# One Strassen level for the gate and up products of two SwiGLU FFNs

## The chip, the core and the metric

The kernel runs on one core of one Trainium2 chip. TensorE (PE) multiplies matrices and writes PSUM, VectorE (DVE), ScalarE (ACT) and GpSimd (POOL) work element by element, SyncE (SP) issues the DMA transfers. The metric is the device time of one execution in microseconds, as the median of several runs.

## What is computed

An inference step of a two-layer decoder: a pooling mixer and an FFN, then a gated DeltaNet mixer and an FFN, each between two RMS norms, on 512 prompt tokens and 64 sample tokens together (T = 576) with 1024 features. The change is about the FFN of both layers:

```python
def swiglu(h, w_in, w_out):
    gu = h @ w_in                                  # 1024 x (2 x 2816)
    return (jax.nn.silu(gu[..., :D_FF]) * gu[..., D_FF:]) @ w_out

for i in range(DEPTH):
    h = rms_norm(x, norm_mix_pre[i])
    ...
    x = x + rms_norm(m, norm_mix_post[i])
    h = rms_norm(x, norm_ffn_pre[i])
    x = x + rms_norm(swiglu(h, ffn_w_in[i], ffn_w_out[i]), norm_ffn_post[i])
```

## The kernel before

**Layout.** Activations lie with features on the 128 partitions (8 chunks) and tokens along the free dimension. The tokens are cut into two halves (`HALVES`): A with 256 columns and B with 320, with PSUM banks 0 to 2 and 3 to 5 (tags A and B, so `ps_A` and `ps_B`).

**Arithmetic.** Every large product is made of three matmuls on float32r: an operand is split into a rounded part (`wh`, `hH`, `aH`, made by an ACT copy) and the rest (`wl`, `hL`, `aL`, a subtraction on DVE or GpSimd). `mm3` (L663) adds wh x hH, wh x hL and wl x hH for each chunk. `Weights` (L645) loads a block of 1024 x 128 weights as one DMA into `wraw` (three slots) and splits it into `wh` and `wl` (three slots each).

**The FFN** (`ffn`, L759). The hidden layer has 22 slices of 128, in blocks of 8, 7 and 7 (`FBLOCKS`). A slice is a pair: a gate block and an up block of w_in, 8 chunks each. A block's slices are followed by eight output tiles (`y`), products with w_out that are summed over the blocks. The first pairs of each FFN, its head (14 chunks, 7 pairs, in layer 0, 10 chunks, 5 pairs, in layer 1), run for half A and then again for half B, with the weights loaded twice, since B's norm is not done yet; the last eight output tiles do likewise, so that A's norm can begin before B is done. Between them each weight block is used for both halves. The residual x stays in SBUF through each FFN; in layer 1 it is transposed on PE beside the pairs (`turn_x`, L1721) into `xT`, to which the turned output is added.

**Between the layers** x goes to DRAM (`x_d`), since the mixer of layer 1 needs its room. That mixer's output product is made in two parts: the first is put away in DRAM (`y_d`), the second is added behind the mixer (L1699 to L1710), where `y_d` and `x_d` come back in one transfer for each half.

**The order.** The kernel's calls are not issued as they are written. `Plan` (L51) records them with their dependences, and `forward` (L339) sets an order for each engine from estimated durations, several times over with changed priorities; the best is issued. An operation marked `EITHER` goes to DVE or GpSimd. Where the planner expects PE to wait for long it puts fillers there, matmuls on ones into an unused bank (`ps_w`, issued at L279; two records each in the trace). On its engine each queue runs in order; SP's DMA issues too. All recorded operations have one line in the profile, L283.

Of the kernel before, what the change touches and what calls it, by code (L numbers as in the profile page):

```python
# [11 lines left out]
F32 = mybir.dt.float32  # L12
# [38 lines left out]
class Plan:  # L51
# [16 lines left out]
    LEAVE, KEEP = 0.3, 1.0  # L68
    ROUNDS, STIR, SEED = 40, (0.0, 0.0, 300.0, 1000.0, 3000.0), 2
# [4 lines left out]
    def start(self):  # L74
        self.on = True
        self.ops, self.last, self.tags = [], {}, {}
        self.gone, self.ends, self.home, self.after = set(), set(), {}, {}
        self.banks, self.holds = {}, {}

    class Engine:  # L80
        def __init__(self, plan, real):
            self.plan, self.real = plan, real

        def __getattr__(self, method):
            def put(*a, **k):
# [47 lines left out]
    @staticmethod  # L133
    def meet(a, b):
        return a[0] < b[1] and b[0] < a[1] and a[2] & b[2] != 0

# [51 lines left out]
    def put(self, method, calls, a, k):  # L188
# [10 lines left out]
        for x, write in [(x, False) for x in ins] + [(x, True) for x in outs]:  # L199
# [20 lines left out]
            for q, w in log:  # L220
                if (write or w) and q[0] != i and self.meet(r, q[1]):
                    preds.add(q[0])
            log.append(((i, r), write))
# [115 lines left out]
    def forward(self, rank):  # L339
# [65 lines left out]
        while todo:  # L405
# [23 lines left out]
            if e == "POOL":  # L429
# [5 lines left out]
                if not mine:  # L435
# [4 lines left out]
                    continue  # L440
            elif e == "DVE" and port["POOL"] > t + 300:
# [57 lines left out]
def hybrid_kernel(  # L499
# [12 lines left out]
        ("PE", nc.tensor), ("ACT", nc.scalar), ("DVE", nc.vector), ("POOL", nc.gpsimd), ("SP", nc.sync)))  # L512
    EITHER = plan.engine(DVE=nc.vector, POOL=nc.gpsimd)
# [41 lines left out]
    hv = [None, None]  # L555

    def new_h(hi):
        hv[hi] = [hp.tile([P, NC, HALVES[hi][1]], F32R, name="h%s%d" % (x, hi), tag="h%s%d" % (x, hi), bufs=1)
                  for x in "HL"]

    for hi in range(2):
        new_h(hi)
# [4 lines left out]


    sp = pool("gsmp")

    bet = sp.tile([P, SP1, VH], F32, name="bet")
    gH = sp.tile([P, SP1, VH], F32R, name="gH")
    gL = sp.tile([P, SP1, VH], F32R, name="gL")
    gce = sp.tile([P, SP1, VH], F32, name="gce")
    gcq = sp.tile([P, SP1, VH], F32, name="gcq")
    ngc = sp.tile([P, SP1, VH], F32, name="ngc")
    kde = sp.tile([P, SP1, VH], F32, name="kde")
    gls = sp.tile([P, NB, VH], F32, name="gls")
    glp = sp.tile([P, SPANS, VH], F32, name="glp")
    rq = sp.tile([P, SP1, KH], F32, name="rq")  # L580
    nk = sp.tile([P, SP1, KH], F32, name="nk")
# [63 lines left out]
    class Weights:  # L645
# [98 lines left out]
    def pre_norm(tp, x, acc, hi, gpre, on_dve=False):  # L744
        o0, n = HALVES[hi]
        r = rstd(tp, acc, hi, on_dve)
        for c in range(NC):
            t = halftile(tp, "nh", hi, 2)
# [4 lines left out]
    def post_pre(tp, x, m, acc, hi, gpost, gpre, fast=False):  # L753
        acc2 = []
        post_norm(tp, x, m, acc, hi, gpost, acc2, (DVE, POOL) if fast else (POOL,), hi == 1)
        pre_norm(tp, x, acc2, hi, gpre, hi == 1)


    def ffn(layer, y, wts, ap_, tp, head, tail, finish, beside=None, turn=None):  # L759
# [3 lines left out]
        chunks = []  # L763
        f0 = 0
        for bi, nb in enumerate(FBLOCKS):
            for f in range(nb):
                chunks.append(("g", bi, f, f0, nb))
                chunks.append(("u", bi, f, f0, nb))
            for m in range(NC):
                chunks.append(("y", bi, m, f0, nb))  # L770
            f0 += nb
# [1031 lines left out]
```

## Time and profile before

| what | value |
| --- | --- |
| median of 3 runs | 1650.28 us |
| their range | 1646.72 to 1653.22 us |
| span of the profiled execution (its own time is given as this alone) | 1654.1 us |
| mean granted clock of PE over the span | 0.989 |

A line of the profile names an engine, an operation and its tiles (written <- read), with buffer numbers left out. PE's matmuls overlap, so their pace is read from start to start. The stages by time: pooling mixer and norms to about 60 us, FFN of layer 0 to about 490, mixer of layer 1 to about 1140, its output product to about 1190, FFN of layer 1 to the end.

### The profile page before, as it was taken

How to read it: one execution, taken by the hardware profiler on the slowest of the kernel's cores; microseconds unless marked ns; L12 is line 12 of the kernel's file. 1: busy time of each engine (PE TensorE's matmuls, PEld its weight loads, DVE VectorE, ACT ScalarE, POOL GpSimd, SP SyncE). 2: the span in 40 equal slices, each digit the busy share in tenths (PEclk: the TensorE clock that was granted, in tenths of full speed). 3: DMA queues.
4: the chain of work that ended last, by engine and by line, in shares of the span. 5: the costliest groups of instructions: out<-in, count | busy, mean ns of one | idle time of the engine just before them, and what ended most of it. 6: DMA issues, size and time to landing. Idle time of an engine off the chain costs nothing. (4 is left out here: it accounts for less than half of the span.)

```text
span 1654.1 us, 30525 instructions
## 1 busy us (share of the span) xinstructions
PE 1620.4 (98%) x12317; PEld 1567.2 (95%) x12317; DVE 1002.7 (61%) x2074; ACT 699.4 (42%) x1434; POOL 119.5 (7%) x265
## 2 busy tenths in 40 slices
PE   8999999999999999999999999999999999999997
PEld 8999999999999998998898899899999999999997
DVE  6784223333387798997998899656694312233244
ACT  6653233212365944553453554424464322222244
POOL 3010000000001010021121131100000000000000
PEclk8899999999999999999999999999999999999999
DMA  6255322223366233324323423557544323223333
GB/s 175 67 157 146 90 77 81 86 77 90 92 171 167 84 104 93 100 75 137 89 77 104 116 78 116 163 167 244 171 135 135 102 75 92 72 79 92 87 102 113
DMA packets 329812, 185.25 MB, mean 112 GB/s; under 512 B 12235, under 2 KB 324140, under 8 KB 329407
## 3 DMA queue, kind: packets, MB, share of 16 engines
q1 hardware_dynamic: 329671, 183.30, 38.2%
q8 instruction: 97, 1.59, 0.4%
q14 instruction: 44, 0.36, 0.1%
HBM read 157.73 MB, written 25.77 MB: 111 GB/s over the span
## 5 line engine op out<-in xcount | busy, mean ns | idle before, releaser
L283 DVE TENSOR_TENSOR wl<-wraw,wh 128x1024 fp32r<-128x1024 f32 (+2 forms) x253 | 301.9, 1201 | 292.1 <-PE ps_A L283 102.6
L283 ACT ACTIVATE wh<-wraw 128x1024 fp32r<-128x1024 f32 (+2 forms) x259 | 266.4, 1035 | 481.5 <-PE ps_A L283 185.9
L283 PE MATMUL ps_m<-hH,wh 128*128 128x256 f32 (+1 forms) x832 | 239.1, 309 | 1.4 <-ACT zz L283 1.2
L283 PE MATMUL ps_m<-hL,wh 128*128 128x256 f32 (+1 forms) x832 | 238.9, 308 | 0.0
L283 PE MATMUL ps_m<-hH,wl 128*128 128x320 f32 (+1 forms) x832 | 236.7, 309 | 0.0
L283 PE MATMUL ps_B<-hL,wh 128*128 128x320 f32 x768 | 224.2, 311 | 0.3 <-DVE hL L283 0.3
L283 PE MATMUL ps_B<-hH,wl 128*128 128x320 f32 x768 | 223.9, 311 | 0.1
L283 PE MATMUL ps_B<-hH,wh 128*128 128x320 f32 x768 | 223.3, 311 | 0.3 <-ACT sg L283 0.3
L283 PE MATMUL ps_A<-hH,wh 128*128 128x256 f32 x768 | 205.6, 285 | 1.3 <-DVE yo L283 1.3
L283 PE MATMUL ps_A<-hL,wh 128*128 128x256 f32 x768 | 204.1, 284 | 0.0
L283 PE MATMUL ps_A<-hH,wl 128*128 128x256 f32 x768 | 202.7, 284 | 0.1
L283 PEld LDWEIGHTS ps_m<-hH,wh 128*128 128x128 f32 x832 | 152.5, 190 | 6.5 <-ACT zz L283 1.8
L283 PEld LDWEIGHTS ps_m<-hL,wh 128*128 128x128 f32 x832 | 152.5, 190 | 2.2 <-DVE hL L283 0.2
L283 PEld LDWEIGHTS ps_m<-hH,wl 128*128 128x128 f32 x832 | 151.8, 190 | 2.8 <-issue 0.9
L283 PEld LDWEIGHTS ps_A<-hH,wh 128*128 128x128 f32 x768 | 142.8, 191 | 2.3 <-issue 1.4
L283 PEld LDWEIGHTS ps_A<-hL,wh 128*128 128x128 f32 x768 | 142.7, 191 | 0.2
L283 PEld LDWEIGHTS ps_A<-hH,wl 128*128 128x128 f32 x768 | 141.8, 191 | 0.4 <-DVE wl L283 0.2
L283 PEld LDWEIGHTS ps_B<-hL,wh 128*128 128x128 f32 x768 | 141.2, 189 | 0.6 <-DVE hL L283 0.5
L283 PEld LDWEIGHTS ps_B<-hH,wl 128*128 128x128 f32 x768 | 141.2, 189 | 0.5 <-DVE wl L283 0.2
L283 PEld LDWEIGHTS ps_B<-hH,wh 128*128 128x128 f32 x768 | 140.4, 189 | 0.9 <-ACT sg L283 0.5
L283 PE MATMUL ps_B<-aH,wh 128*128 128x320 f32 x352 | 102.1, 311 | 0.0
L283 PE MATMUL ps_B<-aL,wh 128*128 128x320 f32 x352 | 102.0, 310 | 0.0
(388 smaller groups left out, 3109.1 us busy)
## 6 DMA issues: line engine op xcount, KB each, us to landing
wraw<-in_ffn_w_in_dram SPq DMA_DIRECT2D x112, 512.0 KB
wraw<-in_gdn_w_in_dram SPq DMA_DIRECT2D x56, 512.0 KB
wraw<-in_ffn_w_out_dram SPq DMA_DIRECT2D x48, 448.0 KB
wraw<-in_gdn_w_out_dram SPq DMA_DIRECT2D x24, 512.0 KB
wraw<-in_ffn_w_out_dram SPq DMA_DIRECT2D x16, 512.0 KB
St<-in_state_gdn_rec_dram SPq DMA_DIRECT2D x32, 256.0 KB
out_dram<-St SPq DMA_DIRECT2D x32, 256.0 KB
z_d<-zz SPq DMA_DIRECT2D x16, 288.0 KB
```

The source lines that it names most:

```text
L283: calls[e](*a, **k)
```

## The change

**Products.** The tokens are also cut into two equal parts N1 and N2 of 288 columns, the features into two halves K1 and K2 of four chunks. Behind the heads, whose sizes stay, a pair is seen as a 2 x 2 block matrix (gate and up by K1 and K2) times a 2 x 2 block matrix (K1 and K2 by N1 and N2). `seven` multiplies them by the Strassen-Winograd scheme with seven block products (`part`, four chunks of three matmuls on 288 columns each) in three PSUM banks. The sums of weights that it needs are made for each pair from the raw weights and split like weights: `ws` (split into `wh`, `wl`), the changed up block (`th`, `tl`, one slot) and half of the changed gate block (`qh`, `ql`, one slot). The sums of results are added on DVE between the products: `su` is up, `sg` gate.

**Activations.** The sums of activations are made once for each FFN: `twist` writes them over the normed activations, which `pre_norm` now leaves in y, and splits them into `tH` and `tL` (`TW`). `hH` and `hL` become one tile for both halves.

**x.** `tH` takes x's place in SBUF. So x goes to a DRAM tile `x_m` before the pairs and comes back for the last pass; in layer 1 its transposition moves there too, and `xT` takes the place of `tL`.

**Transfers.** x and y move in pieces by feature chunk. Those marked `BULK` wait in the planner while it expects the DMA queue to be over `QUEUE` further behind. The small tiles of the mixer of layer 1 (`gsmp`) exist during that mixer only.

```diff
+N1, N2 = slice(0, T // 2), slice(T // 2, T)
+K1, K2 = slice(0, NC // 2), slice(NC // 2, NC)
+HEADS = (7, 5)
...
+            elif e == "SP" and dma > t + 1400 + self.QUEUE:
+                mine = [x for x in q if not taken[x[1]] and x[1] not in self.bulk]
+                if not mine:
+                    soon = [r[0][0] for r in (ready[e],) if r and r[0][0] > t]
+                    free[e] = max(t + 50.0, min(soon + [dma - 1400 - self.QUEUE]))
...
+    HT = [hp.tile([P, NC, T], F32R, name="h%s" % x) for x in "HL"]
+    hv = [[h[:, :, o0:o0 + n] for h in HT] for o0, n in HALVES]
+    x_m = dp.tile([P, NC, T], F32, name="x_m")
...
-        def load(self, src, row, col, nk, n=P, eng=EITHER):
+        def raw_of(self, src, row, col, nk, n=P):
             raw = self.p.tile([P, 8, P], F32, name="wraw", tag="wraw", bufs=self.raw)[:, :nk, :n]
             SP.dma_start(raw, src[row:row + nk * P, col:col + n].rearrange("(k p) m -> p k m", p=P))
-            return self.split(raw, eng)
-
-        def split(self, raw, eng=EITHER):
+            return raw
+
+        def load(self, src, row, col, nk, n=P, eng=EITHER):
+            return self.split(self.raw_of(src, row, col, nk, n), eng)
+
+        def split(self, raw, eng=EITHER, p=None, tag="w", bufs=None):
             _, nk, n = raw.shape
-            h = self.p.tile([P, 8, P], F32R, name="wh", tag="wh", bufs=self.bufs)[:, :nk, :n]
-            l = self.p.tile([P, 8, P], F32R, name="wl", tag="wl", bufs=self.bufs)[:, :nk, :n]
+            full = 8 if p is None else nk
+            h, l = ((p or self.p).tile([P, full, P], F32R, name=tag + x, tag=tag + x, bufs=bufs or self.bufs)[:, :nk, :n]
+                    for x in "hl")
...
+    def twist(Y, TW):
+
+        for a, b in ((0, 2), (2, 4)):
+            top, low = Y[:, a:b], Y[:, 4 + a:4 + b]
+            EITHER.tensor_tensor(top[:, :, N1], top[:, :, N2], top[:, :, N1], op=sub)
+            EITHER.tensor_tensor(top[:, :, N2], low[:, :, N2], top[:, :, N2], op=sub)
+            EITHER.tensor_tensor(low[:, :, N2], low[:, :, N2], top[:, :, N1], op=sub)
+            EITHER.tensor_tensor(low[:, :, N1], low[:, :, N1], low[:, :, N2], op=sub)
+            for c in range(a, b):
+                for k in (c, 4 + c):
+                    split2(Y[:, k], TW[0][:, k], TW[1][:, k])
...
+        def part(ps, w, k0, src, ks, cols, first):
+            wh, wl = w
+            for j, k in enumerate(range(ks.start, ks.stop)):
+                hi_, lo = (t[:, k, cols] for t in src)
+                PE.matmul(ps, wh[:, k0 + j], hi_, start=first and j == 0, stop=False, skip_group_check=True)
+                PE.matmul(ps, wh[:, k0 + j], lo, start=False, stop=False, skip_group_check=True)
+                PE.matmul(ps, wl[:, k0 + j], hi_, start=False, stop=j == 3, skip_group_check=True)
+
+        def seven(f, ring):
+
+            rg, ru = (wts.raw_of(*win_of(kind, f)) for kind in "gu")
+            w0 = wts.split(rg)
+            ws = ap_.tile([P, 8, P], F32, name="ws", tag="ws", bufs=1)
+            EITHER.tensor_tensor(ws[:, K1], ru[:, K1], ru[:, K2], op=add)
+            EITHER.tensor_tensor(ws[:, K2], ws[:, K1], rg[:, K1], op=sub)
+            w1 = wts.split(ws)
+            EITHER.tensor_tensor(ru[:, K1], rg[:, K1], ru[:, K1], op=sub)
+            w2 = wts.split(ru, p=ap_, tag="t", bufs=1)
+            EITHER.tensor_tensor(rg[:, K2], rg[:, K2], ws[:, K2], op=sub)
+            w3 = wts.split(rg[:, K2], p=ap_, tag="q", bufs=1)
+            a, b, c = (bank(ring)[:, :T // 2] for _ in range(3))
+            sg = ap_.tile([P, T], F32, name="sg", tag="sg", bufs=2)
+            u = ap_.tile([P, T], F32, name="su", tag="su", bufs=2)
+            part(a, w0, 0, HT, K1, N1, True)
+            ACT.activation(u[:, N1], a, AF.Copy)
+            part(c, w1, 0, TW, K1, N1, True)
+            part(b, w1, 4, TW, K2, N2, True)
+            DVE.tensor_tensor(sg[:, N2], u[:, N1], b, op=add)
+            part(a, w0, 4, HT, K2, N1, False)
+            ACT.activation(sg[:, N1], a, AF.Silu)
+            part(b, w2, 0, TW, K1, N2, False)
+            DVE.tensor_tensor(u[:, N2], u[:, N1], b, op=add)
+            DVE.tensor_tensor(u[:, N2], u[:, N2], c, op=add)
+            part(c, w3, 0, HT, K2, N2, False)
+            DVE.tensor_tensor(sg[:, N2], sg[:, N2], c, op=add)
+            ACT.activation(sg[:, N2], sg[:, N2], AF.Silu)
+            part(b, w2, 4, TW, K2, N1, False)
+            DVE.tensor_tensor(u[:, N1], u[:, N1], b, op=add)
+            gated(f, sg, u, slice(0, T))
...
+        for hi in range(2):
+            for f in range(head):
+                plain(f, hi)
+        for bi, (f0, nb) in enumerate(blocks):
+            for f in range(max(f0, head), f0 + nb):
+                seven(f, "AB"[f % 2])
+            if bi == last:
                 ACT.activation(warm, eps_c, AF.Sqrt)
-            if i == len(chunks) - 1:
-                finish(hi, s["acc"])
-
-        n = len(chunks)
-        last_silu = n - NC - 2
-        for lo, hi in ((0, head), (n - tail, n)):
-            if lo:
-                for i in range(head, lo):
-                    w = load(i)
-                    run(i, 0, w)
-                    run(i, 1, w)
-                    if beside is not None and i >= 2 * head:
-                        next(beside, None)
-            for half in range(2):
-                for i in range(lo, hi):
-                    run(i, half, load(i))
+                more = back()
+                for hi in range(2):
+                    for m in range(NC):
+                        for _ in range(2):
+                            next(more, None)
+                        out(bi, m, hi, wts.load(wout, f0 * P, m * P, nb))
+            else:
+                for m in range(NC):
+                    w = wts.load(wout, f0 * P, m * P, nb)
+                    for hi in range(2):
+                        out(bi, m, hi, w)
...
+                for c in range(NC):
+                    BULK.dma_start(x_m[:, c, o0:o0 + n], x[:, c, o0:o0 + n])
...
+            TW = [xp.tile([P, NC, T], F32R, name="tH", tag="x", bufs=1), ap_.tile([P, NC, T], F32R, name="tL")]
+            twist(Y, TW)
+            xs = []
+
+            def back0():
+                x = xp.tile([P, NC, T], F32, name="x", tag="x", bufs=1)
+                xs.append(x)
+                for o0, n in HALVES:
+                    for c in range(NC):
+                        BULK.dma_start(x[:, c, o0:o0 + n], x_m[:, c, o0:o0 + n])
+                return iter(())
...
-    for hi, (o0, n) in enumerate(HALVES):
-        SP.dma_start(y[o0], y_d[hi])
     for hi, (o0, n) in enumerate(HALVES):
         acc = []
         for m in range(NC):
+            BULK.dma_start(y[o0][:, m], y_d[hi][:, m])
+            BULK.dma_start(x[:, m, o0:o0 + n], x_d[:, m, o0:o0 + n])
             ps = bank("AB"[hi])[:, :n]
-            if m == 3:
-                SP.dma_start(x[:, :, o0:o0 + n], x_d[:, :, o0:o0 + n])
             mm3(ps, wts.load(wo, 8 * P, m * P, 8), h_of(hi), 8)
             yc = y[o0][:, m]
             DVE.tensor_tensor(yc, yc, ps, op=add)
             add_sq(tp, acc, yc, m, hi)
-        new_h(hi)
         post_pre(tp, x, y, acc, hi, G_MPOST + NC, G_FPRE + NC, True)
+        for c in range(NC):
```

The whole order is planned anew. Three places of it, without row numbers.

DVE, in the middle of layer 0's pairs (`wl` and `wraw` of one pair, `sg` and `aL` of the pairs whose products are done). Before, the operations of one pair's length:

```order
L283 TENSOR_TENSOR wl_697<-wraw_695,wh_696 128x1024
L283 TENSOR_TENSOR sg_663<-sg_663,ps_B_672 128x320
L283 TENSOR_TENSOR aL_674<-sg_663,aH_673 128x320
L283 TENSOR_TENSOR wl_706<-wraw_704,wh_705 128x1024
L283 TENSOR_TENSOR sg_680<-sg_680,ps_A_688 128x256
L283 TENSOR_TENSOR aL_690<-sg_680,aH_689 128x256
```

Now, from the last reader of a raw slot (`ql_665` reads `wraw_655`) to the sums of the next pair (`wraw_676` gate, `wraw_677` up, which is loaded into the slot of `wraw_655`):

```order
L295 TENSOR_TENSOR ql_665<-wraw_655,qh_664 128x512
L295 TENSOR_TENSOR sg_672<-su_673,ps_B_669 128x288
L295 TENSOR_TENSOR tl_663<-wraw_656,th_662 128x1024
L295 TENSOR_TENSOR su_652<-su_652,ps_A_648 128x288
L295 TENSOR_TENSOR sg_651<-sg_651,su_652 128x576
L295 TENSOR_TENSOR ws_680<-wraw_677 128x512
L295 TENSOR_TENSOR ws_680<-ws_680,wraw_676 128x512
L295 TENSOR_TENSOR su_673<-su_673,ps_B_669 128x288
L295 TENSOR_TENSOR wraw_676<-wraw_676,ws_680 128x512
L295 TENSOR_TENSOR su_673<-su_673,ps_B_671 128x288
L295 TENSOR_TENSOR wl_682<-ws_680,wh_681 128x1024
L295 TENSOR_TENSOR wraw_677<-wraw_676,wraw_677 128x512
```

Behind these follow, up to the next `ql`, a 576-wide `aL`, a 1024-wide `wl`, a 288-wide `sg` and `ql` itself: 15 operations from one `ql` to the next, all on DVE, where six stood before.

PE, within one pair now (`ps_B_625`, `627` and `629` are its banks a, b and c):

```order
L295 MATMUL ps_B_629<-tL_336,wh_618 128x288
L295 MATMUL ps_B_625<-hH_97,wh_615 128x288
L295 MATMUL ps_B_629<-tH_335,wl_619 128x288
L295 MATMUL ps_B_625<-hL_98,wh_615 128x288
L295 MATMUL ps_B_625<-hH_97,wl_616 128x288
L295 MATMUL ps_B_625<-hH_97,wh_615 128x288
L295 MATMUL ps_B_627<-tH_335,th_620 128x288
L295 MATMUL ps_B_627<-tL_336,th_620 128x288
```

Bank b is written again here (`ps_B_627<-tH_335,th_620`), which waits for the addition `sg_630<-su_631,ps_B_627` on DVE; between the two uses of the bank PE has the other products.

SP, where the FFN of layer 1 is entered (`yo` and `x1` come back, `wraw` are blocks of the output weights). Before:

```order
L283 DMA wraw_2825<-in_gdn_w_out_dram 128x8x128
L283 DMA yo0_2787<-y_d0_104 128x2048
L283 DMA yo256_2788<-y_d256_105 128x2560
L283 DMA x1_2789<-x_d_101 128x8x256
L283 DMA x1_2789<-x_d_101 128x8x320
L283 DMA wraw_2831<-in_gdn_w_out_dram 128x8x128
L283 DMA wraw_2837<-in_gdn_w_out_dram 128x8x128
```

Now:

```order
L295 DMA wraw_2799<-in_gdn_w_out_dram 128x8x128
L295 DMA wraw_2793<-in_gdn_w_out_dram 128x8x128
L295 DMA yo_2750<-y_d0_103 128x256
L295 DMA wraw_2825<-in_gdn_w_out_dram 128x8x128
L295 DMA yo_2750<-y_d0_103 128x256 x7
L295 DMA yo_2750<-y_d256_104 128x320 x3
L295 DMA x1_2751<-x_d_100 128x256 x4
L295 DMA wraw_2831<-in_gdn_w_out_dram 128x8x128
```

The two blocks that stood behind the four transfers (half A's last two) stand ahead of the first piece, and the pieces have half B's weight loads between them. The order has 102 fillers before and 86 now; here the 3, 20, 26 and 2 become 20, of the others 51 become 66.

More of the change, by code (lines that the diff above doesn't have):

```diff
@@ L135, in meet, with inside @@
         return a[0] < b[1] and b[0] < a[1] and a[2] & b[2] != 0
+    @staticmethod
+    def inside(a, b):
+        return b[0] <= a[0] and a[1] <= b[1] and a[2] & ~b[2] == 0
     @staticmethod
@@ L222, in put @@
                     preds.add(q[0])
+            if write and x.space == SB:
+                log[:] = [q for q in log if not self.inside(q[0][1], r)]
             log.append(((i, r), write))
@@ L755, in post_pre @@
         post_norm(tp, x, m, acc, hi, gpost, acc2, (DVE, POOL) if fast else (POOL,), hi == 1)
[L756 to L781 removed]
+        pre_norm(tp, x, acc2, hi, gpre, m, hi == 1)
@@ new lines, in ffn, with win_of, act_of, gated @@
+    def ffn(layer, y, wts, ap_, tp, head, TW, back, finish, turn=None):
+        win, wout = ffn_w_in[layer], ffn_w_out[layer]
+        blocks, f0 = [], 0
+        for nb in FBLOCKS:
+            blocks.append((f0, nb))
+            f0 += nb
+        last = len(blocks) - 1
+        state = [dict(acc=None, turn=None) for _ in HALVES]
+        acts = {}
+        def win_of(kind, f):
+            return win, 0, (f if kind == "g" else DFF // P + f) * P, NC
+        def act_of(f):
+            if f not in acts:
+                acts[f] = [ap_.tile([P, T], F32R, name="a" + x, tag="a" + x, bufs=8) for x in "HL"]
+            return acts[f]
+        def gated(f, sg, u, cols):
+            aH, aL = (a[:, cols] for a in act_of(f))
+            DVE.tensor_tensor(sg, sg, u, op=mult)
+            ACT.activation(aH, sg, AF.Copy)
+            EITHER.tensor_tensor(aL, sg, aH.bitcast(F32), op=sub)
+        def plain(f, hi):
+            o0, n = HALVES[hi]
+            cols = slice(o0, o0 + n)
+            sg = ap_.tile([P, T], F32, name="sg", tag="sg", bufs=2)[:, cols]
+            for kind in "gu":
+                ps = bank("AB"[hi])[:, :n]
+                mm3(ps, wts.load(*win_of(kind, f)), h_of(hi), NC)
+                if kind == "g":
+                    ACT.activation(sg, ps, AF.Silu)
+            gated(f, sg, ps, cols)
+        def part(ps, w, k0, src, ks, cols, first):
[35 more added lines that the diff above has]
+            gated(f, sg, u, slice(0, T))
+        def out(bi, m, hi, w):
+            f0, nb = blocks[bi]
@@ new lines, in out @@
+            yc = y[o0][:, m]
+            if bi == 0:
+                ACT.activation(yc, ps, AF.Copy)
+            else:
+                DVE.tensor_tensor(yc, yc, ps, op=add)
+            if bi == last:
+                if m == 0:
+                    s["acc"] = []
+                add_sq(tp, s["acc"], yc, m, hi)
+                if turn is not None:
+                    if s["turn"] is not None:
+                        next(s["turn"], None)
+                    s["turn"] = turn(hi, m)
+                    next(s["turn"])
+                    if m == NC - 1:
+                        next(s["turn"], None)
+                if m == NC - 1:
+                    finish(hi, s["acc"])
```

140 lines of the change are left out of this document (56 added, 84 removed).

## The prediction

> **What bounds the kernel now.** I read the page first, for the engine that is full.
>
> ```profile
> span 1654.1 us, 30525 instructions
> PE 1620.4 (98%) x12317; PEld 1567.2 (95%) x12317; DVE 1002.7 (61%) x2074; ACT 699.4 (42%) x1434; POOL 119.5 (7%) x265
> PE   8999999999999999999999999999999999999997
> DVE  6784223333387798997998899656694312233244
> ```
>
> The first two lines are the span and the busy times; the slices show that TensorE (PE) is full from end to end, while VectorE (DVE) is full only in the middle, in the mixer of layer 1. Next I read the stretches that the change touches, beside that mixer (600 to 1050 us).
>
> ```profile
> core 0: us, PE busy (x) PEld busy (x) DVE busy (x) ACT busy (x) POOL busy (x), PEclk, DMA share, GB/s
> 60.00:150.00 90.00, 89.67 (x659) 88.41 (x659) 64.17 (x125) 46.49 (x77) 4.41 (x5) 0.98 0.49 143
> 200.00:450.00 250.00, 250.00 (x1886) 250.00 (x1885) 76.99 (x113) 67.56 (x107) 0.00 (x0) 1.00 0.28 81
> 600.00:1050.00 450.00, 434.50 (x3583) 402.85 (x3582) 405.86 (x961) 213.99 (x531) 69.28 (x139) 0.99 0.35 99
> 1200.00:1250.00 50.00, 49.95 (x390) 48.98 (x389) 45.66 (x101) 31.53 (x56) 3.54 (x3) 1.00 0.47 138
> 1300.00:1550.00 250.00, 250.00 (x1881) 249.83 (x1881) 75.91 (x110) 66.96 (x109) 0.00 (x0) 1.00 0.29 85
> 1600.00:1650.00 50.00, 45.69 (x332) 42.96 (x330) 28.68 (x49) 26.73 (x51) 0.00 (x0) 1.00 0.38 116
> ```
>
> Behind the heads of both FFNs (200 to 450, 1300 to 1550) PE never idles, the granted clock is 1.00, and DVE works 30% of the time. There fewer or shorter matmuls are worth their whole time, until something else fills up. 250 us over 1886 matmuls is 132.6 ns each, start to start.
>
> **The pair: PE.** A pair is the gate and up column block for one 128-wide slice of the hidden layer. Before, it takes 2 x 8 x 3 matmuls on 256 columns and as many on 320, 96 in all. Now seven products of 4 x 3 matmuls on 288 columns, 84. No row has 288 columns; the neighbours in the timeline do:
>
> ```profile
> 250.03 0.28 PE L283 MATMUL ps_A<-hH,wh 128*128 128x256 f32 x1
> 250.15 0.31 PE L283 MATMUL ps_B<-hL,wh 128*128 128x320 f32 x1
> 250.30 0.28 PE L283 MATMUL ps_A<-hL,wh 128*128 128x256 f32 x1
> 250.42 0.31 PE L283 MATMUL ps_B<-hH,wl 128*128 128x320 f32 x1
> ```
>
> From a start (first column) to the next is 0.12 us after 256 columns and 0.15 after 320. 288 lies halfway, so I take the mean of the stage, 132.6 ns: 96 x 0.1326 = 12.73 us before, 84 x 0.1326 = 11.14 after, 1.59 less. Heads of 7 and 5 pairs stay as they are, so 15 + 17 = 32 pairs change: **-50.9 us**. With the ends of the bracket, 0.12 and 0.15, a pair would save 2.65 or 0.13 us, 85 or 4 in all; the straight line is why I stay at the middle.
>
> The Trainium skill (TensorE: Matmul & The Clock Gate, Back-to-back issue gap) gives N/2.4 + 2.5 ns for a warm matmul by itself, 122.5 at 288 columns; the same edit would then be worth 32 x 12 x 0.1225 = 47 us. At 256 columns it gives 109 ns where the trace has 0.12 us, so the measurement stands.
>
> **The pair: DVE.** This is the price. Before, DVE does six operations a pair (two weight residuals, two multiplications, two residuals of the activations). Now 15, by the order: three on 1024 elements (wl twice, tl), five on 512 (four sums of weights, ql), five on 288 with PSUM, two on 576. All stand on DVE, none on GpSimd.
>
> ```profile
> L283 DVE TENSOR_TENSOR wl<-wraw,wh 128x1024 fp32r<-128x1024 f32 x204 | 249.7, 1231 | 276.7 <-PE ps_A L283 95.6 <-ACT wh L283 59.8 <-issue 33.1
> L283 DVE TENSOR_TENSOR St<-St,ps_s 128x512 f32<-128x512 f32 x32 | 21.6, 682 | 2.1 <-PE ps_s L283 1.9
> L283 DVE TENSOR_TENSOR sg<-sg,ps_B 128x320 f32<-128x320 f32 x44 | 21.3, 485 | 80.0 <-PE ps_B L283 79.9
> L283 DVE TENSOR_TENSOR sg<-sg,ps_A 128x256 f32<-128x256 f32 x44 | 18.4, 418 | 70.8 <-PE ps_A L283 70.8
> 1142.09 3.49 DVE L283 TENSOR_TENSOR wl<-wraw,wh 128x1024 fp32r<-128x1024 f32 x3
> L283 ACT ACTIVATE wh<-wraw 128x1024 fp32r<-128x1024 f32 x210 | 221.3, 1058 | 393.3 <-PE ps_A L283 134.8 <-PE ps_B L283 102.5 <-PE ps_m L283 68.1
> L283 ACT ACTIVATE aH<-sg 128x320 fp32r<-128x320 f32 x44 | 20.7, 470 | 41.6 <-DVE sg L283 41.4
> ```
>
> The mean ns of one stands behind the busy time: 1231, 682, and between 485 and 418 the 452 of 288 columns; 576 on the line from 512 to 1024 is 751. Sum: 3 x 1.231 + 5 x 0.682 + 5 x 0.452 + 2 x 0.751 = 10.86 us. The row at 1142.09 shows three operations of 1.23 us in 3.49 us, so the next one starts about 0.1 us before the last one's end: 15 of them take 9.4 us back to back. So **DVE fills 84 to 97% of PE's 11.14 us**, where it was at 30%. On ACT a pair has 3.5 weight copies of 1024 elements (3.5 x 1.058 = 3.7 us), three short operations like the 0.470 row and one of 576: under 6 us, half of the pair.
>
> The Trainium skill (VectorE: DVE Perf Modes, The DRAIN you can't avoid) states that the next operation does not start until the pipe is empty; by that a pair would cost DVE the full 10.86 us. The 3.49 us row speaks against it.
>
> Two things make DVE wait as well. The raw weights have three slots and a pair holds two of them, so the load of the next up block is issued only after ql, the last reader of the slot. How long a load takes is seen here:
>
> ```profile
> 261.61 0.37 SPq L283 DMA_DIRECT2D wraw<-in_ffn_w_in_dram  x1
> 264.00:264.50 0.50, 0.50 (x6) 0.50 (x5) 0.00 (x0) 0.00 (x0) 0.00 (x0) 1.00 1.00 300
> 264.50:265.00 0.50, 0.50 (x6) 0.50 (x5) 0.00 (x0) 0.27 (x1) 0.00 (x0) 1.00 0.13 37
> ```
>
> Issued at 261.6, its bytes have come by 264.6 (share 1.00, then 0.13): 3.0 us. Meanwhile DVE has, by the order, sg, tl, su and sg, 0.45 + 1.23 + 0.45 + 0.75 = 2.9 us. Then the whole chain of sums stands behind the load, and behind it on the same in-order queue the additions on PSUM for which PE waits before it may write that bank again. So engine and load turn once in 3.0 + about 0.4 for issue and waking + (9.4 to 10.9 - 2.9) = 9.9 to 11.4 us, beside PE's 11.14: level with it. What PE loses beside so full a DVE two rows tell: 0.05 of 50 us where DVE is at 91% (1200 to 1250), 15.5 of 450, 3.4%, where it is at 90% and often full (600 to 1050). The handshakes resemble the second: 3.4% of 32 x 11.14 = 356 us is **+12 us**; ends 0.4 and, if DVE sets the pace, the second rival below.
>
> **The entry into layer 1's FFN.** Here y and x come back from DRAM in four big transfers before, in 32 pieces now.
>
> ```profile
> 1142.49 0.83 PE L279 MATMUL ps_w<-ones 128*128 128x128 f32 x6
> 1146.11 4.62 PE L279 MATMUL ps_w<-ones 128*128 128x128 f32 x40
> 1152.02 0.35 PE L283 MATMUL ps_A<-hH,wh 128*128 128x256 f32 x1 [1.28 <-DVE yo L283]
> 1160.72 5.96 PE L279 MATMUL ps_w<-ones 128*128 128x128 f32 x52
> 1166.76 0.61 PE L279 MATMUL ps_w<-ones 128*128 128x128 f32 x4
> 1143.94 1.09 SPq L283 DMA_DIRECT2D yo<-y_d  x2
> 1145.08 6.25 SPq L283 DMA_DIRECT2D x<-x_d  x2
> 1151.45 1.08 DVE L283 TENSOR_TENSOR yo<-yo,ps_A 128x256 f32<-128x256 f32 x3 [1.61 <-DMA yo<-y_d]
> ```
>
> ps_w are fillers, matmuls on ones where the planner expects PE to wait. PE loses 0.83 + 4.62 + 1.28 + 5.96 + 0.61 = 13.3 us: first for y, issued at 1143.94 and there at 1151.4, then for weights queued behind x. In the order the 20 fillers (40 records) stay, the 26 (52) go, and all of this half's weights are issued ahead of the first piece of y. Elsewhere, above all in layer 1's mixer, which is planned anew with the rest though no line of its arithmetic changes, the order has 66 fillers for 51, 15 x 2 x 0.1155 = 3.5 us (4.62 us over 40 records is 0.1155). So 13.3 - 4.6 - 3.5: **-5 us**. Ends: -13 if the pieces come early and the rest waits less, 0 if they delay weights instead.
>
> **The transfers of x and the twist.** The twist adds 16 DVE operations on 576 (12 us) and 8 ACT copies in each head; in 60 to 150 DVE has 26 us idle, which hides it; without this cover it costs up to 12. x goes to DRAM in the head and comes back in the last pass: 2.36 MB each way, at the 300 GB/s of the row above 8 us, while the DMA share there is 0.49 and 0.38. On SP's in-order queue the return waits for the last pair's matmuls to release its slot; the loads of wout for the remaining tiles stand behind, PE waits for them, and the four or five wout blocks issued ahead cover it. I take **+2 us**, ends 0 and 28 (12 + 2 x 8, both heads' and returns' cover gone).
>
> **Sum.** 1654.1 - 50.9 + 12.3 - 5 + 2 = 1612.5 us. The profiled execution's own time is given as its span only; it lies 0.23% above the median of the runs, so on their scale 1612.5 x 1650.28/1654.1 = **1608 us**.
>
> **Rivals.**
> - *The gain comes whole* (PE loses 0.4, the entry 13, no cost elsewhere): 1654.1 - 50.9 + 0.4 - 13 = 1590.6, 1587 on the runs' scale. For: 49.95 of 50 beside a DVE at 91%. Against: three slots, one loop. 0.08.
> - *DVE sets the pace.* Full durations 10.86, 0.5 for the load, 0.8 for two hand-overs from ACT: 12.2 us a pair, saving 0.53 x 32 = 17: 1654.1 - 17 - 5 + 2 = 1634, 1630. For: 97% by full durations. Against: the overlap in the 3.49 us row. 0.18. The DRAIN rule of the Trainium skill would lead here.
> - *The transfers and the twist lose their cover*: +28 in place of +2: 1638.5, 1635. 0.08.
> - *Slower: the slot loop.* If a load takes longer than 3.0 us, DVE stands still and PE behind it. With 3.0 us the loop is at most 11.4; it passes the old 12.73 when the load takes over 4.3 us. At 5 us it is 13.4, 0.67 x 32 = 21 us more: 1654.1 + 21 - 5 + 2 = 1672, 1668. For: y took 7.4 us when much was queued. Against: the DMA share in this stage is 0.28. 0.10.
> - The forecast has 0.56.
>
> The change does do what it says: the order has 84 matmuls a pair.
>
> **Range and chances.** 1592 to 1642 leaves out the slower rival and half of the first. What a measurement of this kernel can tell from no change is about 0.5%, 8 us. Faster: 0.56 + 0.08 + 0.16 + 0.06 = 0.86; within: 0.05; slower: 0.09.
>
> **What would show it.** Right: a stretch of pairs with 84 matmuls in 11.2 to 11.7 us, DVE busy 85 to 97%, PE waits of some tenths of a us for DVE's su, sg, tl or wl; the 52 filler records gone. Wrong: 288 columns pacing off 0.13 us; DVE waiting on wraw's DMA for over 1 us a pair; PE waiting for x or wout in the last passes; PE's clock below 1.00 in the pairs.

## The result, and the profile after

| | before | after |
|---|---|---|
| median of 4 runs each | 1649.63 us (1646.72 to 1653.22) | 1608.78 us (1607.29 to 1609.98) |
| ratio | | 0.9749, 95% interval 0.9732 to 0.9765 |
| span of the profiled execution | 1654.1 us | 1605.2 us |
| mean granted clock of PE | 0.989 | 0.989 |

The first lines of the page of the changed kernel, with the slices of PE and DVE:

```profile
span 1605.2 us, 30246 instructions
PE 1567.4 (98%) x11901; PEld 1509.0 (94%) x11901; DVE 1210.6 (75%) x2392; ACT 768.5 (48%) x1516; POOL 130.5 (8%) x267
PE   8999999999999999999999899999999999999998
DVE  6995368568785896997999699757598835846865
```

PE is as full as before with 416 fewer records of matmuls (384 are the pairs' own, 32 x 12, and 32 are fillers), and DVE is now busy in all stages. The stretches that the prediction looked at, in the changed kernel (time from and to; length, then busy time of PE, PEld, DVE, ACT and POOL with instructions; granted clock, DMA share, GB/s):

```profile
60.00:150.00 90.00, 89.20 (x660) 87.61 (x660) 70.77 (x129) 48.37 (x78) 11.14 (x9) 1.00 0.56 163
200.00:450.00 250.00, 249.87 (x1886) 248.52 (x1885) 175.60 (x267) 103.42 (x154) 1.23 (x2) 1.00 0.37 107
1300.00:1550.00 250.00, 250.00 (x1885) 248.96 (x1885) 164.68 (x246) 98.52 (x147) 0.00 (x0) 1.00 0.33 94
```

Behind the heads PE still hardly idles (0.13 us of 500), and its pace is what it was: 1886 and 1881 matmuls in 250 us before, 1886 and 1885 now, though most of them now have 288 columns in place of 256 and 320.

To see where the time went I cut both executions at the same instructions: FFN of layer 0 (first matmul into ps_A on hH to the first into ps_e), mixer of layer 1 (first to last matmul into ps_m), and the last stage (from there to the end, with the FFN of layer 1). The three windows of the kernel before:

```profile
59.10:493.80 434.70, 434.25 (x3238) 432.43 (x3238) 191.95 (x329) 156.08 (x254) 6.86 (x8) 0.99 0.37 106
528.80:1134.60 605.80, 589.57 (x4668) 549.75 (x4667) 515.81 (x1195) 299.69 (x729) 81.33 (x161) 0.99 0.38 109
1134.60:1654.10 519.50, 509.44 (x3833) 504.14 (x3831) 226.37 (x389) 185.32 (x319) 8.55 (x8) 1.00 0.38 113
```

and of the changed one:

```profile
56.40:465.70 409.30, 408.37 (x3049) 404.82 (x3050) 285.57 (x466) 180.42 (x285) 16.73 (x17) 1.00 0.42 122
500.00:1119.60 619.60, 601.09 (x4717) 557.85 (x4716) 520.88 (x1213) 308.32 (x741) 74.45 (x153) 0.99 0.38 108
1119.60:1605.20 485.60, 475.17 (x3560) 469.65 (x3559) 333.68 (x551) 220.56 (x356) 13.07 (x12) 0.99 0.44 130
```

The FFN of layer 0 lost 25.4 us (15 pairs at 1.59 are 23.9) and the last stage 33.9 (17 pairs are 27.0; 6.9 more). So the two FFN stages gained 59 us. But **the mixer of layer 1, of which no line of arithmetic is changed, takes 13.8 us longer**. The rest of the span (ahead of the FFN, and the product into ps_e) gave 3.4. These windows come from one execution each: that of the kernel before, with its span of 1654.1 us, lies above all four runs, that of the change is the fastest of its four, so the spans differ by 48.9 us where the medians differ by 40.9. Two questions followed: what the pairs cost beyond their matmuls, and what lengthened the mixer.

In the mixer PE has 49 more records. These two rows are the fillers in it, before and (second fence) after:

```profile
L279 PE MATMUL ps_w<-ones 128*128 128x128 f32 x42 | 6.0, 280 | 0.0
```

```profile
L291 PE MATMUL ps_w<-ones 128*128 128x128 f32 x64 | 9.1, 275 | 0.0
```

22 of the 49 are fillers, 19 are products for the gates that moved over the stage's border. At the stage's pace, 601.09 / 4717 = 0.127 us, the 49 are 6.2 us; PE's idle time grew from 16.2 to 18.5. The granted clock has a share in the other 5.3. In the mixer it falls to 0.50 for short stretches: two before (606.23 to 609.65 and 770.07 to 776.90 us), 10.2 us together, three after (545.73 to 552.56, 617.41 to 620.82, 893.89 to 900.72), 17.1 us. The first of the three with the time behind it, matmuls from both, and (last fence) the longer one before:

```profile
545.73:552.56 6.83, 6.83 (x25) 5.70 (x26) 6.10 (x11) 6.73 (x11) 0.47 (x2) 0.50 0.28 77
552.56:559.39 6.83, 6.83 (x44) 6.35 (x43) 4.97 (x17) 5.16 (x9) 0.00 (x0) 1.00 0.11 43
```

```profile
549.37 0.41 PE L295 MATMUL ps_m<-hH,wh 128*128 128x256 f32 x1
549.58 0.41 PE L295 MATMUL ps_m<-hL,wh 128*128 128x256 f32 x1
...
552.57 0.28 PE L295 MATMUL ps_m<-hL,wh 128*128 128x256 f32 x1
552.69 0.28 PE L295 MATMUL ps_m<-hH,wl 128*128 128x256 f32 x1
```

```profile
770.07:776.90 6.83, 6.83 (x102) 6.37 (x99) 1.98 (x3) 1.42 (x3) 0.52 (x1) 0.50 0.55 156
```

Inside it matmuls on 256 columns start 0.21 us apart, just behind it 0.12. Half the length of such stretches is an estimate of what they cost, 5.1 us before and 8.5 after, so 3.4 of the 13.8. The clock is not a fixed part of an order: 50 executions of the kernel before, beside the experiments, took 1645.99 to 1660.54 us at clocks between 0.999 and 0.987. The last 2 us stay without a name. Whether the order is what differs, the runs with other orders tell (below).

### The profile page after: what moved, and what is told of

Same layout as the page of the kernel before. It is cut to its first block, busy times and chain, and to the rows that moved or that the text cites. A ratio compares the mean times of both kernels' runs of the same rounds, so it can differ in the third digit from the quotient of the medians.

```text
span 1605.2 us, 30246 instructions
## 1 busy us (share of the span) xinstructions
PE 1567.4 (98%) x11901; PEld 1509.0 (94%) x11901; DVE 1210.6 (75%) x2392; ACT 768.5 (48%) x1516; POOL 130.5 (8%) x267
## 4 chain that ended last, share of the span: by engine, by line
PE 74%; DVE 15%; ACT 4%; DMA 4%; issue 2%; POOL 0%; SPq 0%; DVEq 0%; ACTq 0%
PE ps_B L295 29%; PE ps_A L295 21%; PE ps_m L295 10%; PE ps_s L295 5%; PE ps_k L295 5%; DVE ii L295 2%; DVE wl L295 2%; DMA wraw<-in_ffn_w_in_dram 2%; DVE ac L295 2%; PE ps_e L295 2%; DVE Uw L295 1%; PE ps_x L295 1%; PE ps_n L295 1%; DVE ia L295 1%; DVE vt L295 1%
## 5 line engine op out<-in xcount | busy, mean ns | idle before, releaser
L295 ACT ACTIVATE wh<-wraw 128x1024 fp32r<-128x1024 f32 (+1 forms) x227 | 233.2, 1031 | 266.5 <-PE ps_B L295 93.1
L295 PE MATMUL ps_m<-hH,wh 128*128 128x320 f32 (+1 forms) x832 | 245.5, 311 | 2.1 <-ACT zz L295 1.6
L295 PE MATMUL ps_m<-hL,wh 128*128 128x320 f32 (+1 forms) x832 | 243.9, 309 | 0.0
L295 PE MATMUL ps_B<-hH,wh 128*128 128x320 f32 (+1 forms) x392 | 113.1, 306 | 0.5 <-ACT wh L295 0.5
L295 PE MATMUL ps_B<-hL,wh 128*128 128x320 f32 (+1 forms) x392 | 112.7, 305 | 0.0
L295 PE MATMUL ps_B<-hH,wl 128*128 128x320 f32 (+1 forms) x392 | 111.8, 305 | 0.2 <-DVE wl L295 0.2
L295 PE MATMUL ps_A<-hH,wh 128*128 128x256 f32 (+1 forms) x376 | 103.0, 289 | 2.7 <-DVE yo L295 2.1
L295 PE MATMUL ps_A<-hL,wh 128*128 128x256 f32 (+1 forms) x376 | 102.7, 288 | 0.0
L295 PE MATMUL ps_A<-hH,wl 128*128 128x256 f32 (+1 forms) x376 | 101.9, 289 | 0.1
L295 PE MATMUL ps_B<-aH,wl 128*128 128x320 f32 x352 | 101.0, 312 | 0.1
```

What stands on the lines that cost most here:

```text
L295: calls[e](*a, **k)
```

## The experiments

The runs come in three groups: the pairs' price (e1 to e4), the entry into layer 1's FFN (e5, e13), and the order (e6 to e11). Runs e2, e3 and e4 are one execution each.

**e1_pairs_plain: all of the change but the seven products.**

```diff
             for f in range(max(f0, head), f0 + nb):
-                seven(f, "AB"[f % 2])
+                both(f)
```

`both` multiplies a pair in 96 matmuls as before, on the new tiles; twist, transfers and pieces stay.

> All of the change kept (x out and back, twist, pieces, one tile for h), only the pairs behind the heads multiplied as before, with 96 matmuls on 256 and 320 columns; the twisted activations are made and not used. Stages are read between the first matmul of the first FFN, the first of the mixer's projection (ps_e), the first and last of ps_m, and the end; the changed kernel has 409.3, 34.3, 619.6 and 485.6 us there. Theory A (the gain is the matmuls of the pairs, 1.59 us each, and nothing of it is lost beside them): the first FFN 15 x 1.59 = 24 us longer, 433, and from the last ps_m to the end 17 x 1.59 = 27 longer, 513. Theory B (the pairs lose some 3% to VectorE and the rest of the change makes up for it): 7 us less in each, 426 and 506. Theory C (the gain comes from the transfers and the new order): both within 8 us of the changed kernel. The mixer may move by 15 us either way, since it is planned anew.

Measured: 1650.67 us (1645.94 to 1653.1, 5 runs), ratio to before 0.9986 (0.9944 to 1.0028). Its three windows:

```profile
56.30:489.40 433.10, 431.51 (x3239) 429.76 (x3237) 196.30 (x332) 158.63 (x258) 14.76 (x16) 1.00 0.39 115
520.80:1142.50 621.70, 601.39 (x4721) 558.36 (x4720) 519.39 (x1215) 307.41 (x742) 68.00 (x149) 0.99 0.38 108
1142.50:1651.30 508.80, 499.79 (x3749) 495.35 (x3747) 231.01 (x398) 187.87 (x322) 15.02 (x14) 0.99 0.42 124
```

Layer 0's FFN with twist and transfers takes 433.1 us against 434.7: these cost nothing that shows. The last stage is 10.7 us shorter than before without any pair being cheaper, and the mixer is 15.9 longer. So the gain at the entry and the loss in the mixer both come without the seven products. From e1 to the change the FFN stages lose 23.8 and 23.2 us, 47.0 together.

**e2_one_more and e3_three_more: more work for DVE in each pair.** In e3 three residuals are computed twice (3.4 us); e2 has only the last of these lines (1.2 us):

```diff
             w0 = wts.split(rg)
+            DVE.tensor_tensor(w0[1], rg, w0[0].bitcast(F32), op=sub)
...
             w1 = wts.split(ws)
+            DVE.tensor_tensor(w1[1], ws, w1[0].bitcast(F32), op=sub)
...
             w2 = wts.split(ru, p=ap_, tag="t", bufs=1)
+            DVE.tensor_tensor(w2[1], ru, w2[0].bitcast(F32), op=sub)
```

> The changed kernel with one more operation on 1024 elements on VectorE in each pair: tl is computed twice, and the products wait for the second. Theory overlap (operations start 0.1 us before the last one's end): 9.4 + 1.13 = 10.5 us a pair, under PE's 11.14, so the first FFN stays at 409 within 4 us and the second at 486 within 6. Theory full durations: 10.86 + 1.23 = 12.1 us, 0.95 over PE's: 14 us more in the first FFN (423) and 16 in the second (502).

> The changed kernel with three more operations on 1024 elements on VectorE in each pair (both wl and tl computed twice). Theory overlap: 9.4 + 3.4 = 12.8 us a pair, 1.66 over PE's 11.14: the first FFN 25 us longer, 434, the second 28, 514. Theory full durations: 10.86 + 3.69 = 14.55: 51 and 58 us longer, 460 and 544. Theory slack (VectorE catches up in the output tiles, where it is idle): under 10 us in each.

Measured: e2 1607.29 us, layer 0's FFN 413.5, last stage 481.4, so 4.2 more and 4.2 less than the change: one more operation a pair costs nothing that shows. e3 1612.64 us, 418.8 and 497.4: 9.5 and 11.8 more, 0.6 to 0.7 us a pair for 3.4 us of work. A window among the pairs of e3, and DVE's timeline in it:

```profile
350.00:410.00 60.00, 58.98 (x436) 57.53 (x436) 60.00 (x84) 25.38 (x39) 0.00 (x0) 1.00 0.30 87
```

```profile
371.55 0.68 DVE L295 TENSOR_TENSOR ws<-ws,wraw 128x512 f32<-128x512 f32 x1
372.15 0.68 DVE L295 TENSOR_TENSOR wraw<-wraw 128x512 f32<-128x512 f32 x1
372.75 0.68 DVE L295 TENSOR_TENSOR wraw<-wraw,ws 128x512 f32<-128x512 f32 x1
373.35 0.75 DVE L295 TENSOR_TENSOR aL<-sg,aH 128x576 fp32r<-128x576 f32 x1
374.02 1.22 DVE L295 TENSOR_TENSOR wl<-ws,wh 128x1024 fp32r<-128x1024 f32 x1
375.16 0.68 DVE L295 TENSOR_TENSOR ql<-wraw,qh 128x512 fp32r<-128x512 f32 x1
...
383.01 0.44 DVE L295 TENSOR_TENSOR su<-su,ps_A 128x288 f32<-128x288 f32 x1
383.37 0.68 DVE L295 TENSOR_TENSOR wraw<-wraw 128x512 f32<-128x512 f32 x1
```

Here DVE is full, 60.00 of 60, and each operation starts before the last one's end: 0.60 us from start to start for an operation of 0.68, 0.67 for 0.75, 1.14 for 1.22, 0.36 for 0.44. A pair of the change is then 3 x 1.14 + 5 x 0.60 + 5 x 0.36 + 2 x 0.67 = 9.6 us of DVE, 86% of PE's 11.14. The full durations, on which the prediction's rival of a DVE that sets the pace stood, fall. The prediction had named the rule that the next operation does not start until the pipe is empty as leading to them (the Trainium skill, VectorE: DVE Perf Modes, The DRAIN you can't avoid). This chain does not bear that price out, since its starts lie 0.08 us before the ends. When the pipe is empty no row here shows, and the section adds that a next operation which is not held starts earlier; so what falls is the price of full durations, not the rule. With 9.6 + 3.4 = 13.0 us a pair e3 should have lost 1.9 us in each, and lost a third of it; where the rest went is read behind e4.

**e4_load_twice: a longer slot loop.** The up block is loaded twice, about 6 us in place of 3.0:

```diff
             rg, ru = (wts.raw_of(*win_of(kind, f)) for kind in "gu")
+            src, row, col, nk = win_of("u", f)
+            SP.dma_start(ru, src[row:row + nk * P, col:col + P].rearrange("(k p) m -> p k m", p=P))
```

> The changed kernel with the up block of each pair loaded twice, one load behind the other, so that the slot is filled after 6 us instead of 3. Theory slot loop: load, issue and the operations of VectorE behind it take 6.0 + 0.4 + 6.5 = 12.9 us a pair, 1.8 over PE's 11.14: the first FFN 27 us longer, 436, the second 30, 516. Theory no loop (other pairs' work and the order hide it): both within 6 us.

Measured: 1630.33 us; layer 0's FFN 422.9, last stage 497.1, so 13.6 and 11.5 us more. What the first users of the raw weights waited for, in the view of that tile: in the change

```profile
  DMA wraw<-in_ffn_w_in_dram: 37.3, 19
```

and in e4

```profile
  DMA wraw<-in_ffn_w_in_dram: 64.0, 27
```

The loop of slots and loads is there, but 3 us more in it cost 0.7 to 0.9 us a pair. By the prediction's loop of 9.9 to 11.4 us it would be 12.9 to 14.4 now, above the 12.73 of a pair before, and e4 slower than the kernel before; it is 20 us faster. A stage is a coarse measure for this (layer 0's FFN moves by 10 us between orders of the unchanged work, table below), but whole groups of seven pairs tell more. From the first to the last matmul on 288 columns in the last block of layer 0, in the change, in e3 and in e4:

```profile
332.60:418.50 85.90, 85.90 (x651) 85.80 (x650) 69.39 (x107) 37.53 (x56) 0.00 (x0) 1.00 0.33 96
```

```profile
333.50:424.10 90.60, 89.58 (x668) 88.06 (x667) 87.10 (x123) 37.27 (x55) 0.00 (x0) 1.00 0.30 87
```

```profile
338.20:432.50 94.30, 92.77 (x691) 90.94 (x691) 66.28 (x102) 35.79 (x54) 0.00 (x0) 1.00 0.40 112
```

Of the matmuls 588 (7 x 84) are the pairs' own; 22 in e3 and 44 in e4 are fillers; the other 58 to 63 are output products that stand among the pairs, about 1.2 us a pair. So a pair has 12.3 us here in the change, not 11.14, and 12.9 in e3, 13.5 in e4. All four such groups in these three executions give 12.0 to 12.3, 12.9 to 13.2 and 13.3 to 13.8 us. In e3 that agrees with DVE's 13.0 a pair, and in e4 it lies within the loop's 12.9 to 14.4. So neither price is shown to be too high: of the excess over 11.14, 1.1 to 1.2 us a pair is time in which PE does output products, and what e3 and e4 lose against the change in this group, 0.7 and 1.2 us a pair, is fillers and waits.

**e5_entry_whole: y and x come back in whole transfers at the entry of layer 1's FFN.**

```diff
     for hi, (o0, n) in enumerate(HALVES):
+        SP.dma_start(y[o0], y_d[hi])
+    for hi, (o0, n) in enumerate(HALVES):
         acc = []
         for m in range(NC):
-            BULK.dma_start(y[o0][:, m], y_d[hi][:, m])
-            BULK.dma_start(x[:, m, o0:o0 + n], x_d[:, m, o0:o0 + n])
             ps = bank("AB"[hi])[:, :n]
+            if m == 3:
+                SP.dma_start(x[:, :, o0:o0 + n], x_d[:, :, o0:o0 + n])
```

> The changed kernel, but at the entry of layer 1's FFN y and the half of x beside it come back in whole transfers, as before the change; in the FFN of layer 0 and in the pairs all stays. Theory E (what the stage after the mixer gained beyond 17 x 1.59 us of pairs, about 7 us, comes from the pieces): that stage is 491 to 495 us instead of 485.6, the time about 1615 us, and PE waits again at the first norm pieces of layer 1's FFN. Rival N (the gain there is from where the plan put its fillers and from the clock): the stage stays at 484 to 488 us and the time at 1609 us.

Measured: 1599.03 us (1596.37 to 1602.6, 4 runs), **9.8 us less than the change**, where Theory E said 6 more. The last stage is 4.4 us longer, 490.0, which lies between the two theories' numbers; but the mixer took 608.2 us in place of 619.6. The edit stands behind the mixer, yet the planner issues everything anew. Neither theory had allowed for that, and the total says nothing about the pieces. This run made the order the main question.

**e6 to e11: the same work in other orders.** One line is changed in either kernel, the seed of the planner's search, and in e9 and e10 its rounds also:

```diff
-    ROUNDS, STIR, SEED = 40, (0.0, 0.0, 300.0, 1000.0, 3000.0), 2
+    ROUNDS, STIR, SEED = 40, (0.0, 0.0, 300.0, 1000.0, 3000.0), 3
```

> The changed kernel with the seed of the planner's search 3 instead of 2: the same work in another order, above all in the mixers. Theory P (the 13.8 us that layer 1's mixer lost are the draw of the search): the mixer takes 605 to 614 us, the FFN's stage stays at 409 and the stage after the mixer at 486, each within 4 us, and the time falls to about 1600 us. Rival S (the changed tiles, one h for both layers, and the transfers of x and y cost the mixer its time in any order): the mixer stays at 617 to 624 us, the time at 1605 to 1612 us.

> As the run with seed 3, with seed 5. Theory P: the mixer takes another time than with seed 2, 605 to 616 us, and the time is 1597 to 1608 us. Rival S: the mixer is 617 to 624 us again. Should the three seeds of the changed kernel stand within 3 us of one another, the draw explains nothing.

> The kernel before with seed 3 instead of 2. Theory P (605.8 us of the mixer was a good draw): its mixer takes 612 to 622 us and the time is 1655 to 1665 us, so that against it the change would gain some 10 us more than against seed 2. Rival S (the old tiles let the mixer run in 606 us): the mixer stays at 603 to 609 us and the time within 4 us of seed 2.

> The changed kernel with 160 rounds of the planner's search instead of 40, and seed 12: the same work in an order that was searched for longer. Theory P (the order of the mixers is worth some 10 us, and a longer search finds a better one): layer 1's mixer takes 600 to 612 us where seeds 2, 3 and 5 had 614.9 to 619.6, the two stages with the FFNs stay within 6 us of 409 and 486, the time is 1588 to 1600 us, under the 1608.8 of seed 2. Rival C (the order's worth is lost on the chip, whose waits the planner doesn't know): the time stays at 1602 to 1610 us.

> The kernel before with the same longer search (160 rounds, seed 12). Theory P: it gains less than the changed kernel does, since its seed 2 was a good draw already: mixer 602 to 612 us, time 1638 to 1650 us. Against the changed kernel under the same search the pairs' price then stands at 45 to 55 us. Rival C: the time stays at 1646 to 1653 us.

> The kernel before with seed 5 of the search. Theory P (605.8 us with seed 2 and 612.1 with seed 3 are draws from the range that the changed kernel's mixers have, 608 to 622): mixer 608 to 620 us, time 1648 to 1662 us. Rival S (something in the change, whatever the draw, lengthens the mixer by some 6 us): mixer 604 to 612 us, time 1645 to 1652 us.

Medians (with seed 2 the kernel before over the 22 runs beside e9 to e11, the change over its 4), and stages of one profiled execution each:

| order | before: median | FFN 0 | mixer | last | after: median | FFN 0 | mixer | last |
|---|---|---|---|---|---|---|---|---|
| seed 2 | 1649.88 | 434.7 | 605.8 | 519.5 | 1608.78 | 409.3 | 619.6 | 485.6 |
| seed 3 | 1649.04 | 434.6 | 612.1 | 518.0 | 1604.10 | 419.4 | 614.9 | 483.6 |
| seed 5 | 1657.53 | 435.2 | 618.1 | 515.6 | 1605.72 | 415.0 | 617.8 | 483.0 |
| 160 rounds, seed 12 | 1655.04 | 437.2 | 616.5 | 516.1 | 1585.79 | 410.1 | 608.5 | 480.5 |
| mean | 1652.9 | 435.4 | 613.1 | 517.3 | 1601.1 | 413.5 | 615.2 | 483.2 |

The windows of the mixer in the last order, before and (second fence) after:

```profile
522.20:1138.70 616.50, 593.24 (x4711) 552.35 (x4710) 522.28 (x1221) 295.82 (x731) 65.32 (x144) 1.00 0.38 108
```

```profile
495.50:1104.00 608.50, 588.41 (x4690) 548.92 (x4689) 526.54 (x1233) 305.85 (x748) 67.44 (x150) 0.99 0.39 111
```

The mixer takes 605.8 to 618.1 us before and 608.5 to 619.6 after; the means differ by 2.1 us, less than the orders do among themselves. With seed 2 the kernel before had its best mixer of the four and the change its worst. The other six plans of changed kernels (e1 to e5, e13) lie between 608.2 and 621.7. By the estimate above, the stretches at a clock of 0.50 cost 5.1, 0, 10.2 and 1.7 us of the mixers before and 8.5, 10.2, 3.4 and 3.4 of those after (in the table's order); without them the means are 608.9 and 608.8. So Rival S (something in the change lengthens the mixer in any order) has no support, and Theory P holds in its main point: the 13.8 us are the draw (what the search happened to find) and, for some 3 us, of the clock in these two executions.

Its forecasts for single runs were poor, though. The change's mixer was to fall to 605 to 614 us with seed 3 and 605 to 616 with seed 5 and came to 614.9 and 617.8, the latter within Rival S's numbers; its three seeds stand within 4.7 us of one another, little more than the 3 that I had set as a limit, also because layer 0's FFN took 10 us more with seed 3 (about half of it in the heads: from 60 to 150 us PE has 624 matmuls there at a clock of 0.96, against 660 at 1.00). The time of the kernel before did not rise with seed 3. And a longer search brought nothing to the kernel before (ratio 1.0023, 1.0007 to 1.004, to its seed 2, with a mixer of 616.5 where 602 to 612 were expected), while it took the change to 1585.79 us (ratio to before 0.961, 0.9589 to 0.9631), below the 1588 expected. That is the fastest version here, below both kernels. Rounds and seed were changed together and once for each kernel, so that the longer search is what helped, and not the seed, is not shown. Over the four orders **the change is worth 51.8 us** (1652.9 - 1601.1), and 41, 45, 52 and 69 us in single ones, so the mean is itself uncertain by some 6 us.

**e13_entry_160_12: whole transfers at the entry, in the other order.** The edit of e5 upon e9.

> Entry into layer 1's FFN in whole transfers, as in the run e5, but with the longer search (160 rounds, seed 12). Theory E (the pieces are worth 4 to 8 us at the entry, and e5 was faster only because its mixer drew 608 us): some 100 filler matmuls of 12 us stand around the entry again (16 of 2.2 us with the pieces under this search), the stage after the mixer takes 486 to 492 us instead of 480.5. Its time is then 1590 to 1596 us if the mixer draws the 608 us of the run with pieces, and more by what it draws above that. Rival W (whole transfers are no worse, or better): the stage after the mixer takes 478 to 484 us, and fillers stand there for under 6 us.

Measured: 1620.13 us (1617.5 to 1621.36, 5 runs), 34.3 more than e9; the last stage 497.0 against 480.5, the mixer 616.7 against 608.5. PE's timeline at the entry in e13, without the products between the rows:

```profile
1132.80 2.39 PE L291 MATMUL ps_w<-ones 128*128 128x128 f32 x20
1134.81 8.87 PE L291 MATMUL ps_w<-ones 128*128 128x128 f32 x78
```

and in e9, where the first piece of y is enough to begin:

```profile
1112.68 1.05 PE L291 MATMUL ps_w<-ones 128*128 128x128 f32 x8
1114.10 0.36 PE L295 MATMUL ps_A<-hH,wh 128*128 128x256 f32 x1 [0.37 <-DVE yo L295]
```

Theory E holds, and more than fully: without the pieces the stage is 16.5 us longer. With e5's 4.4 the pieces are worth some 10 us at the entry, as e1's 10.7 says too. The fillers say the same in every order: in the first 80 us of the last stage stand 84 to 112 records of them with whole transfers (the four orders before, e5, e13) and 4 to 40 with pieces (the four of the change, e1 to e4), on average 78 fewer, 9 us at the 0.1155 us of a record.

## Why the prediction was right

The forecast was 1608 us and the time 1608.78, inside the range. That it is so close is luck. In spans the forecast was 1612.5 and the measurement 1605.2: against its terms the two FFN stages came out 14 us better, the mixer 10 us worse and the rest 3 us better, and the step from span to median, 0.23% down for the kernel before and 0.22% up for the change, hid the 7 us that were left.

- *The pairs' matmuls (-50.9): right.* 84 matmuls at 132.6 ns; the straight line between 256 and 320 columns holds:

```profile
235.80 0.29 PE L295 MATMUL ps_B<-tL,th 128*128 128x288 f32 x1
...
237.91 0.29 PE L295 MATMUL ps_A<-hH,wh 128*128 128x288 f32 x1
```

  16 matmuls in the 2.11 us between these starts are 131.9 ns each, so 84 take 11.1 us, just under the 11.2 to 11.7 that I had named as the sign.
- *PE's loss beside a full DVE (+12): mis-sized.* In the changed kernel PE loses 0.13 of 250 us in layer 0 and nothing in layer 1's 250. Over the four orders layer 0's FFN gained 22.0 of 23.9 us; from e1 to the change both FFNs gained 47.0 of 50.9. So the term is 2 to 4 us, as far as single orders tell. The step that failed is the choice between two rows: I took the mixer's 3.4% because the handshakes resemble it. But the mixer's PE idles in chains of small products that depend on one another, while here the next products' operands lie ready; a busy share of DVE near 90% is not by itself a price. The other row (0.05 of 50 us lost beside a DVE at 91%) was the right one. DVE's 9.4 us a pair were right (9.6 in e3's full stretch), and so was its share among the pairs (52.23 of 60 us, last fence below); the waits of PE for `su`, `sg`, `tl` and `wl` that I had named as the sign of the +12 don't stand out in either 250 us.
- *The slot loop (9.9 to 11.4 us, and the slower rival): mechanism and price agree with e4, what it was held against does not.* e4's groups take 13.3 to 13.8 us a pair where the loop gives 12.9 to 14.4, so in the change it stays below the 12.0 to 12.3 us that a pair has there with the output products. DVE waits for the up block's load, 7.5 us in three waits from 200 to 450 and 10.2 in four from 1300 to 1550, under the 1 us a pair named as a sign, and PE loses nothing by it. The rival was to make the kernel slower than before from a load of 4.3 us on; at about 6 us e4 takes 1630.33 us. It left out that PE has output products to do meanwhile.
- *The entry (13.3 - 4.6 = 8.7 of the -5): right.* The last stage gained 33.9 - 27.0 = 6.9 us in the profiled pair; e1, e5 and e13 put the entry at 4 to 16, the fillers at 9. They went as the order showed: 40 records stay, the 52 are gone. The wait for y's first piece stays as well, 2.09 us behind the 40 records:

```profile
1130.05 4.62 PE L291 MATMUL ps_w<-ones 128*128 128x128 f32 x40
1136.77 0.36 PE L295 MATMUL ps_A<-hH,wh 128*128 128x256 f32 x1 [2.09 <-DVE yo L295]
1130.94 0.45 SPq L295 DMA_DIRECT2D yo<-y_d  x1
```

- *Transfers and twist (+2): nothing.* e1's FFN of layer 0 has them and is 1.6 us shorter than before; in the change DVE works 70.77 of the 90 us from 60 to 150 and PE is busy for 89.20.
- *What was missing: the order of the mixer.* I priced the replanned mixer at 15 fillers, 3.5 us, by counting rows of the order. It lost 13.8. Rows of the order show fillers, not how long the chains between them wait, and one order of the mixer differs from another by up to 14 us in these runs. Nor had I priced the stretches at half clock, which cost a mixer 0 to 10 us by the estimate above. The mixer's loss stood in the place of the +12 that did not come.

The comparison between two single orders hides this: 41 us of gain by the medians, 51.8 over four orders. The latter is what the pairs (-50.9), their small loss (+2 to +4), the entry (-9 to -10) and the mixer (+2.1) add up to, -54 to -57, within some 2 to 5 us; the spans of the four profiled executions give -53.9.

Open is what in an order makes the mixer longer or shorter: of the 13.8 us, more matmul records (fillers above all) and idle time explain 8.5 and the clock about 3.4, but why one order needs more of them, and what lowers the clock, was not tried. e2, e3 and e4 were run once each.

## What to carry to other kernels

Where a search sets the order of the whole program, any edit draws it anew: compare several draws of both kernels, or read the edited stage alone, before a difference of under 1% is put down to the edit. Price fewer matmuls by their pace in the stage itself, and a second engine's load by whether the first engine's next operands are ready, not by its busy share in another stage. When an edit has changed what the search must place, search again: here one other draw, searched for longer, was worth another 23 us to the changed kernel, and nothing to the one before. Before a second engine's or a loop's time is held against the first engine's, count everything that the first one does in that stretch: here a pair had 12.3 us, not 11.14.

## What the runs showed of the hardware

A VectorE that is busy for 60.00 of 60 us ran 83 operations in e3 (350 to 410 us) whose durations, added up from the timeline, are 66.85 us: back to back the next operation starts about 0.08 us before the last one's end, whatever its length between 0.44 and 1.22 us. TensorE's pace on 288 columns lies on the line between 256 and 320 at a clock of 1.00, and it did not fall beside a VectorE at 52.23 of 60 us, in this window of the changed kernel:

```profile
350.00:410.00 60.00, 60.00 (x454) 59.90 (x453) 52.23 (x81) 28.78 (x43) 0.00 (x0) 1.00 0.33 94
```

TensorE's granted clock is not the same throughout an execution: in the mixer it stood at 0.50 for stretches of 3.4 to 13.7 us, with 256-column matmuls about 0.21 us apart in place of 0.12. Over 50 executions of one order the mean granted clock ran from 0.987 to 0.999.
